# GpSimd's elementwise work in the Strassen projections of a hybrid streaming encoder goes to VectorE

## The chip, the cores and the metric

The kernel runs on one core of one Trainium2 chip. A core has five engines with a queue of instructions each, taken in order: TensorE (PE in the profile) multiplies matrices into PSUM, VectorE (DVE), ScalarE (ACT) and GpSimd (POOL) work on elements, and SyncE (SP) issues all DMAs of this kernel. The metric is the device time of one execution in microseconds (us).

## The reference, cut to what matters

Two layers over 1088 tokens (1024 of a prompt, 64 of a sample) with 1024 features in float32. The attentions and the pooling branch are not touched by the change and are left out here.

```python
def layer(x, ple, ...):
    h = rmsnorm(x, norm_in)
    hq, hkv, g_a, u_b, g_b, qkv_c, g_c, g_mix = split_cols(h @ w_in)     # input projection
    o_a, o_b, o_c = three token mixers (latent attention, pooling, chunk attention), each times silu(gate)
    gates = sigmoid(g_mix)
    m = gates[:, :D] * (o_a @ w_o_mla) + gates[:, D:2*D] * (o_b @ w_o_pool) + gates[:, 2*D:] * (o_c @ w_o_ca)
    x = x + m @ w_out                                                    # output projection
    x = x + sigmoid(rmsnorm(x, ple_norm) @ w_ple_gate) * (ple @ w_ple_proj)   # gate projection
    return x
```

## The kernel before, in words

**Tiling.** Features lie on partitions, tokens along the free dimension. Tokens are cut into two halves of H = 544, and a matmul has C = 272 columns. A float32 operand is split into a high part (float32r, a cast on ScalarE, line 108) and a low part (the operand less its high part, `lo`, lines 115 to 121), and each product is three matmuls: high by high, high by low, low by high. So every operand costs a cast on ScalarE and a subtraction on VectorE or GpSimd.

**Products.** `gemm` runs a projection as a sequence of pairs of output tiles. A pair is one level of Strassen-Winograd: seven products in the order of `PROD`, each 24 matmuls in the profile's records, of sums of weights (S1 to S4, made on VectorE in `prep_w`, line 342) with operands B11, B21, B22, T1 to T4. Weights are prepared two products ahead: sum, high part, low part (`wop`). `WLO` names the three weights of a pair (A12, S1, A22) whose low parts GpSimd makes. The running sums U2 and U3 are added on VectorE out of PSUM (line 385); U2<-P1 is the first of them in a pair, two products in, and serves below as the mark of a pair. The pairs of a layer: 22 of the input projection, then, behind the attention, 4 of the output projection and 4 of the gate projection, then the next layer's input projection. Counted through the program they are pairs 0 to 21, 22 to 25, 26 to 29, 30 to 51, 52 to 55 and 56 to 59.

**Boundaries.** The seven operands of a projection are made of four quarters of the eight tiles of x (`operand`, for each of four kb slices: scale by the gains, sum, high and low part). `OPS` gives the engine of each low part: B22 and T2 on GpSimd, B21 and T1 on both in turn where several slices come at once, the others on VectorE. `norm_boundary` (the start, the gate projections, layer 1's input projection) also runs 1/rms: squares on ScalarE, their sum in `acc` on VectorE (line 427), a matmul, a short chain, a transpose (rT), and a DMA through memory that spreads the result over all rows (`rbc`). The results of a norm boundary's products are multiplied by rbc when they leave PSUM. In the merge (`merge`), 16 blocks of the latent attention's projection are multiplied by their gate on VectorE (line 1464), added to the other two branches on GpSimd (line 1465), and turned into the operands of the output projection slice by slice, without gains.

**Order.** The program is recorded by a framework that sets the order of the instructions in each engine's queue by priorities and its own estimates; an engine does not pass over a waiting instruction. Tiles have few buffers: three PSUM buffers for products, four sums U, eighteen halves of x, three weights' operands.

**What the change touches.** `operand` (low parts, scales of line 286), `prep_w` (low parts of weights, line 353), `out` of the output projection (line 677: x + U), `out` of the gate projection (line 710: times rbc; line 714: x plus the gated addend) and `merge` (line 1465).

Of the kernel before, what the change touches and what calls it, by code (L numbers as in the profile page):

```python
# [19 lines left out]
L = 2  # L20
T = 1088            # tokens: prompt 0..1023, sample 1024..1087
H = T // 2          # token half
C = H // 2          # columns of one matmul
KT = 1600           # key tokens: prompt 1024 | cached 512 | sample 64
EPS = 1e-6
NEG = -1e30
SCALE = float(np.float32(96.0) ** np.float32(-0.5))   # of the latent attention

# z tiles (128 features each) of the input projection
# [3 lines left out]
# order of the pairs: those that are normalized lie apart  # L33
W_ORDER = (0, 4, 1, 5, 2, 6, 3, 7, 8, 9) + tuple(range(10, 22))
# gain columns
G_IN, G_PLE, G_Q, G_KV, G_KR, G_QH, G_KN, G_CQ, G_CK, G_PS, NG = 0, 8, 16, 18, 19, 20, 21, 22, 23, 24, 26
# columns that average squares
# [3 lines left out]
SECOND = 10                          # pair from which only merge gates are left  # L41
# tiles of the attention: tag, words, buffers; those that the first head waits for are apart
# [5 lines left out]
# PSUM banks of the parts of a layer  # L48
BANKS = {"gemm": (("pg", 3), ("pn", 2)), "keys": (("pg", 2), ("pn", 2), ("po", 2)),
         "attn": (("pg", 3), ("pn", 2), ("po", 1), ("pv", 2))}  # L50
LATE = 100               # how far work that fills gaps stands back
NEAR, BESIDE = 8, 14    # units before the last one at which later work is put in
PVE = ("v",)
FIRST = (2, 2, 1)         # steps of the work beside the attention that go before it
OV = 0
QC, QM = (8, 0, 1, 2, 3, 4, 5, 6, 7), (2, 3, 6, 7, 8, 0, 1, 4, 5)    # chunks of queries in order
L1, L2 = 1, 5
HEADS = tuple(("c", h) for h in range(4)) + tuple(("m", h) for h in range(8))
NRAW, NX, NZT = 3, 18, 5    # buffers: raw weights, halves of x, z tiles
# the products of an output pair: weights, operand  # L60
PROD = (("A11", "B11"), ("S2", "T2"), ("A12", "B21"), ("S3", "T3"), ("S1", "T1"), ("A22", "T4"), ("S4", "B22"))
WLO = ("A12", "S1", "A22")                         # weights whose low parts GpSimd makes
# operands in the order of their making, with the engines of their low parts
OPS = tuple(zip(("B11", "B22", "T2", "B21", "T3", "T1", "T4"), ("v", "g", "g", "vg", "v", "vg", "v")))


class Pair:
    """Two M tiles of a product: where its weights lie, where its blocks go."""

    def __init__(self, src, out, begin=None, mid=None):  # L70
        self.src, self.out, self.begin, self.mid = src, out, begin, mid


class K:
# [4 lines left out]
    # ---------------------------------------------------------------- tools  # L79
# [43 lines left out]
    def split(self, src, hi, lo, eh="a", el="v", sc=None):  # L123
        """high and low parts of src, or of src * sc"""
        self.hi(hi, src, eh, sc)
        self.lo(lo, src, hi, el, sc)
# [10 lines left out]
    # ---------------------------------------------------------------- set-up  # L137
    def setup(self, es):
# [47 lines left out]
        self.kc_d = f("kc", [2, 2, 128, KT], F32R)       # tile, hi/lo  # L186
# [4 lines left out]
    def banks(self, kind):  # L191
        """pools of PSUM banks, anew for each part of a layer"""
        if self.pes:
            self.pes.close()
        self.pes = es = ExitStack()
        for n, b in BANKS[kind]:
            setattr(self, n, es.enter_context(self.tc.tile_pool(name=n, bufs=b, space=PSUM)))
# [5 lines left out]
    # ---------------------------------------------------------------- 1/rms  # L203
    def rstd(self, sqs, col, ng, dst, w=T):
        """dst[:] <- -2/sqrt(mean square + eps) of each token, on all rows of its group; a generator."""
# [31 lines left out]
    # ---------------------------------------------------------------- operands of a Strassen-Winograd product  # L237
    def bop_tiles(self, es, side):
        """a pool for each, so that the first ones free their place before the last ones are done"""
# [5 lines left out]
    def operand(self, n, f, kbs, el, g=None):  # L245
        """operand n of the kb slices: f[kb] = (b11, b12, b21, b22), overwritten on the way; g: columns of gains"""
        nc = self.nc
        stt = nc.vector.scalar_tensor_tensor
        if n == "B11":
            self.scaled = set()  # L250
        for i, kb in enumerate(kbs):
            b11, b12, b21, b22 = f[kb]
            src = {"B11": b11, "T1": b12, "T2": b22, "B21": b21, "B22": b22, "T3": b11, "T4": b21}[n]
            e = el[i % len(el)]
# [4 lines left out]
            if n == "T2":  # L259
                if g and ("B22", kb) not in self.scaled:  # L260
# [5 lines left out]
            elif n == "T4":  # L266
                if g and ("B21", kb) not in self.scaled:
# [3 lines left out]
            if sc is not None and e == "g":  # L271
                self.scale(src, sc)
                self.scaled.add((n, kb))
                sc = None
            h, lo = (t[:, kb] for t in self.bop[n])
            self.split(src, h, lo, "a", e, sc)
            if n == "B11":
                if sc is not None:
                    self.scale(b11, g1)
                if g:  # L280
                    stt(b12, b12, g1, b11, op0=ALU.mult, op1=ALU.subtract)
# [3 lines left out]
    def scale(self, x, g):  # L285
        self.nc.gpsimd.tensor_scalar(x, x, g, 1.0, op0=ALU.mult, op1=ALU.mult)

    def operands(self, f, kbs, g=None):
        for n, el in OPS:
            self.operand(n, f, kbs, el, g)  # L290
# [5 lines left out]
    # ---------------------------------------------------------------- Strassen-Winograd over a sequence of pairs  # L296
# [3 lines left out]
    def weight_pool(self, es, side):  # L300
        """raw weights and operands of them; before the pools of the part that it is for"""
# [8 lines left out]
    def gemm_begin(self, pairs, early=()):  # L310
        """loads and first operands of the weights; early: places of sums of them"""
# [144 lines left out]
    def start(self):  # L456
        """layer 0: x from the input"""
        x = {}
# [1184 lines left out]
```

## Time and profile before

| | |
|---|---|
| median of 3 runs | 2405.88 us (2403.3 to 2421.93) |
| profiled execution, first to last instruction (span) | 2395.0 us |
| median less this span | 10.9 us |
| PE busy | 2216.3 us (93%) |
| DVE busy | 1838.6 us (77%) |
| POOL busy | 1363.5 us (57%) |
| ACT busy | 1199.8 us (50%) |

The profile records one execution. Busy shares are means over stages with different limits; the sections of the program that the change touches are read by windows of the trace further down.

### The profile page before, as it was taken

To read this page: it belongs to the slowest core of one execution; us is meant where nothing else is said; L and a number is where in the kernel's file an instruction comes from. 1 tells how busy PE (TensorE), PEld (TensorE's weight loads), DVE (VectorE), ACT (ScalarE), POOL (GpSimd) and SP (SyncE) were. 2 spreads that over 40 slices of the span, in tenths; PEclk is the share of its full clock that TensorE was granted. 3 is DMA by queue.
4 is the path that set the end of the run, shared out by engine and by line. 5 is a ranking of instruction groups with operands and counts; after the bars stand their busy time and mean duration, and the time that the engine had idled before them with its cause. 6 is when DMAs were issued, how large, how long until landed. Compare 5 with 4: busy or idle time off the path is not lost.

```text
span 2395.0 us, 44977 instructions
## 1 busy us (share of the span) xinstructions
PE 2216.3 (93%) x16134; PEld 2097.7 (88%) x16134; DVE 1838.6 (77%) x3382; ACT 1199.8 (50%) x2533; POOL 1363.5 (57%) x1326
## 2 busy tenths in 40 slices
PE   4999999999999999897869999999999999998978
PEld 3999999999778999797859999999987789997978
DVE  8666787675677888889996667877756778888897
ACT  5334355454666665344443343654546766743442
POOL 6544545667455545657775354447564555455677
PEclk8999999999899999998969999999989999999989
DMA  3433446355966664434515344554478656655253
GB/s 112 173 117 125 161 151 195 118 163 176 252 186 176 189 184 152 169 131 136 193 59 182 113 143 163 163 155 148 137 201 244 183 171 181 178 178 174 91 164 120
DMA packets 234610, 383.59 MB, mean 160 GB/s; under 512 B 30020, under 2 KB 130708, under 8 KB 234388
## 3 DMA queue, kind: packets, MB, share of 16 engines
q1 hardware_dynamic: 234388, 380.72, 51.0%
q8 instruction: 129, 2.11, 0.4%
q14 instruction: 93, 0.76, 0.1%
HBM read 245.94 MB, written 134.70 MB: 159 GB/s over the span
## 4 chain that ended last, share of the span: by engine, by line
PE 61%; DVE 17%; DMA 7%; issue 7%; POOL 5%; ACT 3%; SPq 1%; POOLq 0%; DVEq 0%; ACTq 0%
PE g L377 35%; PE S L1065 4%; PE pv L884 4%; PE pT L850 4%; PE S L994 3%; DVE S L342 2%; DVE wop L119 2%; PE mps L130 1%; DVE acc L427 1%; PE mps L132 1%; PE mps L131 1%; PE vps L1034 1%; DMA of<-mbo 1%; PE turn L1110 1%; DMA of<-p 1%
## 5 line engine op out<-in xcount | busy, mean ns | idle before, releaser
L644 POOL TENSOR_TENSOR z<-z,rbc 128x544 f32<-128x544 f32 x134 | 207.3, 1551 | 178.4 <-DVE z L643 168.3
L119 POOL TENSOR_TENSOR wop<-wraw,wop 128x512 fp32r<-128x512 f32 (+1 forms) x152 | 208.9, 1375 | 141.1 <-ACT wop L108 138.8
L824 POOL TENSOR_SCALAR P<-P,st 128x640 f32<-128x640 f32 (+8 forms) x216 | 155.2, 722 | 218.6 <-DVE st L823 135.0
L108 ACT CAST wop<-wraw 128x512 fp32r<-128x512 f32 (+1 forms) x230 | 138.7, 604 | 218.2 <-PE g L377 159.9
L108 ACT CAST wop<-S 128x512 fp32r<-128x512 f32 x234 | 144.7, 619 | 164.1 <-PE g L377 156.7
L119 DVE TENSOR_TENSOR wop<-S,wop 128x512 fp32r<-128x512 f32 x176 | 170.0, 966 | 72.0 <-ACT wop L108 70.7
L377 PE MATMUL g<-T1h,wop 128*128 128x272 f32 x960 | 183.6, 304 | 21.3 <-DVE U L385 19.0
L377 PE MATMUL g<-B11h,wop 128*128 128x272 f32 x960 | 176.1, 295 | 18.0 <-ACT B11h L110 11.7
L119 DVE TENSOR_TENSOR PT<-pT,PT 128x512 fp32r<-128x512 f32 (+4 forms) x360 | 167.9, 473 | 30.0 <-ACT PT L108 27.6
L377 PE MATMUL g<-B21h,wop 128*128 128x272 f32 x960 | 181.3, 299 | 9.4 <-ACT P L389 5.3
L377 PE MATMUL g<-T3h,wop 128*128 128x272 f32 x960 | 180.3, 297 | 7.4 <-ACT T3h L108 4.9
L377 PE MATMUL g<-T2h,wop 128*128 128x272 f32 x960 | 178.6, 296 | 8.9 <-ACT T2h L108 6.6
L108 ACT CAST PT<-pT 128x512 fp32r<-128x512 f32 (+4 forms) x360 | 147.7, 419 | 67.2 <-PE pT L850 61.3
L377 PE MATMUL g<-B22h,wop 128*128 128x272 f32 x960 | 172.8, 290 | 7.5 <-DVE U L385 4.7
L377 PE MATMUL g<-T4h,wop 128*128 128x272 f32 x960 | 172.6, 291 | 2.1 <-DVE ev L704 2.1
L884 PE MATMUL pv<-PT,V 128*128 128x256 f32 x928 | 167.3, 301 | 6.0 <-DVE PT L119 5.4
L130 PE MATMUL mps<-oh,wop 128*128 128x272 f32 x512 | 157.1, 308 | 16.2 <-DVE g L1464 9.2
L377 PEld LDWEIGHTS g<-T1h,wop 128*128 128x128 f32 x960 | 150.3, 202 | 24.5 <-issue 14.3
L850 PE MATMUL pT<-ident,P 128*128 128x128 f32 x936 | 160.0, 279 | 3.1 <-DVE PT L119 2.7
L1065 PE MATMUL S<-K,Q 96*128 96x384 f32 (+5 forms) x672 | 158.6, 353 | 3.4 <-ACT P L816 3.3
L377 PEld LDWEIGHTS g<-B11h,wop 128*128 128x128 f32 x960 | 143.6, 194 | 19.4 <-ACT B11h L110 12.0
L377 PEld LDWEIGHTS g<-B21h,wop 128*128 128x128 f32 x960 | 146.7, 196 | 13.3 <-ACT P L389 7.9
(274 smaller groups left out, 6957.0 us busy)
## 6 DMA issues: line engine op xcount, KB each, us to landing
wraw<-win SPq DMA_DIRECT2D x88, 512.0 KB
z<-z SPq DMA_DIRECT2D x96, 272.0 KB
g<-z SPq DMA_DIRECT2D x64, 272.0 KB
z<-z SPq DMA_DIRECT2D x24, 544.0 KB
Q<-q SPq DMA_DIRECT2D x32, 408.0 KB
K<-k SPq DMA_DIRECT2D x32, 400.0 KB
k<-hl SPq DMA_DIRECT2D x48, 256.0 KB
q<-hl SPq DMA_DIRECT2D x64, 192.0 KB
```

Source lines behind the costliest of these rows:

```text
L108: nc.scalar.copy(out, src)
L119: e.tensor_sub(out, src, hi)
L130: mm(ps, lhsT=wh, rhs=xh, start=first, stop=False)
L131: mm(ps, lhsT=wh, rhs=xl, start=False, stop=False)
L342: op(tmp[nm], x, y)
L377: nc.tensor.matmul(ps[:, c, :C], lhsT=hl[:, w, kb, :], rhs=b[:, kb, c * C:(c + 1) * C], start=k == 0 and not more, stop=k == 11, skip_grou ...
L644: nc.gpsimd.tensor_mul(o, o, self.half(self.r, ti))
L824: nc.gpsimd.tensor_scalar(u.p[:, :n], u.p[:, :n], st[:, 4:5], 1.0, op0=ALU.mult, op1=ALU.mult)
L850: nc.tensor.transpose(ps[:, j], p[:, c0:c0 + 128], self.ident)
L884: nc.tensor.matmul(ps[:, :w], lhsT=v(b), rhs=grp[b // 4][:, b % 4, j, :w], start=i + j == 0, stop=i == len(bl) - 1 and j == 1)
L994: nc.tensor.matmul(ps[:, :w], lhsT=q[:, q0:q0 + 128], rhs=k[:q.shape[0], k0 + c * w:k0 + c * w + w], start=q is q1, stop=q is q2)
L1065: nc.tensor.matmul(ps[:, :ww], lhsT=q[0:96, q0:q0 + 128], rhs=k[0:96, k0 + c * w:k0 + c * w + ww], start=i == 0, stop=i == 2 and not diag)
```

## The change

Five kinds of GpSimd instructions go to VectorE: the low parts of the operands at all boundaries, the low parts of the weights A12, S1 and A22 in the output and gate projections and in the first two pairs of each input projection (`calm` is true from the third pair on, where they stay), x + U in the output projection, the two elementwise operations of the gate projection, and the addition in the merge. The scales by gains, which were separate GpSimd instructions, are taken into the instruction that makes the low part or the sum, but for that of B11, which ScalarE does.

```diff
-WLO = ("A12", "S1", "A22")                         # weights whose low parts GpSimd makes
-# operands in the order of their making, with the engines of their low parts
-OPS = tuple(zip(("B11", "B22", "T2", "B21", "T3", "T1", "T4"), ("v", "g", "g", "vg", "v", "vg", "v")))
+WLO = ("A12", "S1", "A22")
+
+OPS = ("B11", "B22", "T2", "B21", "T3", "T1", "T4")
...
-                if g and ("B22", kb) not in self.scaled:
+                if g:
                     stt(b22, b22, g2, b12, op0=ALU.mult, op1=ALU.subtract)
...
-                if g and ("B21", kb) not in self.scaled:
+                if g:
                     stt(b21, b21, m2, b22, op0=ALU.mult, op1=ALU.add)
...
-            if sc is not None and e == "g":
-                self.scale(src, sc)
-                self.scaled.add((n, kb))
-                sc = None
             h, lo = (t[:, kb] for t in self.bop[n])
-            self.split(src, h, lo, "a", e, sc)
+            self.split(src, h, lo, "a", "v", sc)
             if n == "B11":
-                if sc is not None:
-                    self.scale(b11, g1)
                 if g:
+                    nc.scalar.activation(b11, b11, AF.Copy, scale=g1)
                     stt(b12, b12, g1, b11, op0=ALU.mult, op1=ALU.subtract)
...
-        self.split(src, hl[:, 0], hl[:, 1], "a", "g" if n in WLO else "v")
+        self.split(src, hl[:, 0], hl[:, 1], "a", "g" if n in WLO and pairs[p].calm else "v")
...
             if sb is not None:
-                nc.gpsimd.tensor_add(o, o, sb)
+                nc.vector.tensor_add(o, o, sb)
...
-                nc.gpsimd.tensor_mul(t, t, self.half(self.r, ti))
+                nc.vector.tensor_mul(t, t, self.half(self.r, ti))
...
-            nc.gpsimd.tensor_add(o, o, g)
+            nc.vector.tensor_add(o, o, g)
...
-                nc.gpsimd.tensor_add(self.half(mb, ti), self.half(mb, ti), self.half(g, ti))
+                nc.vector.tensor_add(self.half(mb, ti), self.half(mb, ti), self.half(g, ti))
```

The queues change as follows: VectorE has 238 instructions more, GpSimd 278 fewer, ScalarE 16 more; TensorE's count is the same. In the rows below, names are tiles of the program with their buffer numbers, and the line numbers of the changed kernel differ (385 is 374, 1464 is 1453, 1465 is 1454, 678 is 667, 677 is 666, 709 is 698, 710 is 699, 713 is 702).

VectorE at the head of layer 0's merge, before (g0 is a gate, mps the projection in PSUM, mb the sum of the other branches):

```order
L1464 TENSOR_TENSOR g0_11903<-g0_11903,mps_11909 128x544
L1464 TENSOR_TENSOR g0_11903<-g0_11903,mps_11936 128x544
L119 TENSOR_TENSOR wop_12050<-wraw_12048,wop_12050 128x512
L1464 TENSOR_TENSOR g0_11907<-g0_11907,mps_11972 128x544
L119 TENSOR_TENSOR B11l_11867<-mb_11901,B11h_11866 128x544
L283 TENSOR_TENSOR mb_11901<-mb_11901 128x544
```

The same place now:

```order
L1453 TENSOR_TENSOR g0_11897<-g0_11897,mps_11903 128x544
L1453 TENSOR_TENSOR g0_11897<-g0_11897,mps_11930 128x544
L1454 TENSOR_TENSOR mb_11895<-mb_11895,g0_11897 128x544
L119 TENSOR_TENSOR wop_12044<-wraw_12042,wop_12044 128x512
L1454 TENSOR_TENSOR mb_11895<-mb_11895,g0_11897 128x544
L1453 TENSOR_TENSOR g0_11901<-g0_11901,mps_11966 128x544
L119 TENSOR_TENSOR B11l_11861<-mb_11895,B11h_11860 128x544
L275 TENSOR_TENSOR mb_11895<-mb_11895 128x544
```

The additions to mb stand in VectorE's queue between the gates now. From the first of these rows to the next projection's first U2<-P1 there were 67 instructions on VectorE, and there are 93.

VectorE at the end of the boundary from the output to the gate projection, and the first products behind it, before (rt is the copy of the transposed 1/rms ahead of its DMA, ev the gate's block, x the addend and the stream):

```order
L226 COPY rt_13563<-rT_13561 9x128
L119 TENSOR_TENSOR T4l_11892<-x_12986,T4h_11891 128x544
L342 TENSOR_TENSOR S2_13846<-S1_13844,wraw_13663 128x512
L385 TENSOR_TENSOR U3_13725<-U2_13656,g_13700 128x544
L119 TENSOR_TENSOR wop_13766<-S4_13764,wop_13766 128x512
L119 TENSOR_TENSOR wop_13806<-wraw_13663,wop_13806 128x512
L385 TENSOR_TENSOR U2_13656<-U2_13656,g_13730 128x544
L709 TENSOR_TENSOR ev_13756<-U3_13725,g_13730 128x544
L342 TENSOR_TENSOR S3_13924<-wraw_13663 128x512
L709 TENSOR_TENSOR ev_13796<-U3_13725,g_13771 128x544
L119 TENSOR_TENSOR wop_13848<-S2_13846,wop_13848 128x512
L713 TENSOR_TENSOR x_13569<-x_13569,ev_13689 128x544
```

The same place now:

```order
L226 COPY rt_13551<-rT_13549 9x128
L374 TENSOR_TENSOR U3_13713<-U2_13644,g_13688 128x544
L119 TENSOR_TENSOR wop_13794<-wraw_13651,wop_13794 128x512
L331 TENSOR_TENSOR S3_13912<-wraw_13651 128x512
L374 TENSOR_TENSOR U2_13644<-U2_13644,g_13718 128x544
L698 TENSOR_TENSOR ev_13744<-U3_13713,g_13718 128x544
L698 TENSOR_TENSOR ev_13784<-U3_13713,g_13759 128x544
L119 TENSOR_TENSOR wop_13836<-S2_13834,wop_13836 128x512
L699 TENSOR_TENSOR ev_13677<-ev_13677,rbc_87 128x544
L699 TENSOR_TENSOR ev_13744<-ev_13744,rbc_87 128x544
L699 TENSOR_TENSOR ev_13784<-ev_13784,rbc_87 128x544
L702 TENSOR_TENSOR x_13557<-x_13557,ev_13677 128x544
```

The three products with rbc, which stood in GpSimd's queue, stand in VectorE's eight instructions behind the copy that starts rbc's DMA.

## Rows read from the trace of the kernel before

**Rows 1.** The page: the span, and busy time of each engine (share, instructions).

```profile
span 2395.0 us, 44977 instructions
PE 2216.3 (93%) x16134; PEld 2097.7 (88%) x16134; DVE 1838.6 (77%) x3382; ACT 1199.8 (50%) x2533; POOL 1363.5 (57%) x1326
```

**Rows 2.** Windows: start:end, length, busy us and instructions of each engine, clock, DMA.

```profile
core 0: us, PE busy (x) PEld busy (x) DVE busy (x) ACT busy (x) POOL busy (x), PEclk, DMA share, GB/s
9.80:63.40 53.60, 29.75 (x109) 24.54 (x110) 50.07 (x55) 29.53 (x50) 43.12 (x24) 0.80 0.22 83
63.40:97.80 34.40, 34.40 (x267) 34.37 (x267) 21.96 (x28) 12.94 (x20) 21.92 (x15) 0.96 0.60 211
937.20:1005.30 68.10, 56.46 (x412) 53.61 (x410) 66.04 (x68) 24.52 (x41) 44.96 (x27) 0.97 0.44 149
1038.70:1059.70 21.00, 21.00 (x170) 21.00 (x169) 15.91 (x20) 7.50 (x12) 10.76 (x8) 1.00 0.29 104
1044.80:1067.90 23.10, 23.10 (x187) 23.10 (x186) 19.27 (x24) 11.16 (x18) 14.01 (x11) 1.00 0.27 95
1067.90:1116.60 48.70, 36.28 (x218) 34.09 (x218) 48.50 (x51) 23.26 (x40) 39.61 (x22) 0.79 0.36 116
1116.60:1192.10 75.50, 66.82 (x507) 64.98 (x504) 70.09 (x70) 31.64 (x52) 53.96 (x35) 0.98 0.56 186
1192.10:1252.70 60.60, 37.64 (x186) 34.21 (x186) 60.57 (x58) 27.47 (x47) 49.55 (x30) 0.66 0.19 64
2128.50:2196.50 68.00, 56.59 (x413) 53.73 (x412) 65.96 (x68) 24.53 (x41) 45.02 (x27) 0.97 0.51 177
2236.00:2259.10 23.10, 23.10 (x185) 23.10 (x184) 19.05 (x23) 10.70 (x18) 13.70 (x11) 1.00 0.26 94
2259.10:2307.90 48.80, 36.19 (x220) 34.26 (x219) 48.80 (x50) 23.68 (x39) 39.72 (x22) 0.79 0.37 115
2307.90:2374.30 66.40, 62.51 (x493) 61.41 (x492) 55.70 (x59) 22.87 (x38) 47.39 (x31) 1.00 0.47 158
2386.10:2395.00 8.90, 0.02 (x1) 0.00 (x0) 2.59 (x3) 0.96 (x2) 5.31 (x4) 0.76 0.25 94
```

**Rows 3.** Waits of PE, 1083 to 1262 us: who for whom, total, times, longest.

```profile
PE g L377 <- DVE T3l L119: 9.8, 3, 6.4
```

**Rows 4.** Timeline, DVE near the start: start us, duration us, instruction.

```profile
33.53 0.71 DVE L427 TENSOR_TENSOR acc<-acc,sq 128x544 f32<-128x544 f32 x1
34.16 0.71 DVE L263 TENSOR_TENSOR x<-x 128x544 f32<-128x544 f32 x1
...
35.43 0.77 DVE L281 SCALAR_TENSOR_TENSOR x<-x,gh 128x544 f32<-128x544 f32 x1
36.13 0.68 DVE L119 TENSOR_TENSOR wop<-S,wop 128x512 fp32r<-128x512 f32 x1
36.73 0.71 DVE L265 TENSOR_TENSOR x<-x 128x544 f32<-128x544 f32 x1
```

**Rows 5.** Timelines of DVE, then of POOL, at the boundary to the gate projection.

```profile
1098.98 1.87 DVE L270 TENSOR_TENSOR x<-x 128x544 f32<-128x544 f32 x1
1100.77 1.85 DVE L263 TENSOR_TENSOR x<-x 128x544 f32<-128x544 f32 x1
...
1098.44 1.83 POOL L119 TENSOR_TENSOR B22l<-x,B22h 128x544 fp32r<-128x544 f32 x1
1100.23 1.81 POOL L119 TENSOR_TENSOR T2l<-x,T2h 128x544 fp32r<-128x544 f32 x1
```

**Rows 6.** Groups by line: instruction, count, busy us, mean ns, idle before it.

```profile
L385 DVE TENSOR_TENSOR U<-U,g 128x544 f32<-128x544 f32 x120 | 85.7, 715 | 49.5 <-PE g L377 49.0
L342 DVE TENSOR_TENSOR S<-wraw 128x512 f32<-128x512 f32 x118 | 112.3, 951 | 40.9 <-POOL wop L119 37.1 <-DMA wraw<-win 1.6 <-DMA wraw<-wout 0.9
L1465 POOL TENSOR_TENSOR mb<-mb,g 128x544 f32<-128x544 f32 x32 | 54.3, 1706 | 44.6 <-DVE g L1464 44.6
L710 POOL TENSOR_TENSOR ev<-ev,rbc 128x544 f32<-128x544 f32 x26 | 43.2, 1671 | 33.3 <-DVE ev L709 17.7 <-DMA rbc<-rd 15.5
```

**Rows 7.** Timelines of DVE, then of POOL: the copy that starts rbc's DMA, its first use.

```profile
1119.23 0.27 DVE L226 COPY rt<-rT 9x128 f32<-9x128 f32 x1
...
1126.54 4.00 POOL L710 TENSOR_TENSOR ev<-ev,rbc 128x544 f32<-128x544 f32 x3 [7.79 <-DMA rbc<-rd]
```

More of the change, by code (lines that the diff above doesn't have):

```diff
@@ L62, with __init__ @@
 WLO = ("A12", "S1", "A22")
-OPS = tuple(zip(("B11", "B22", "T2", "B21", "T3", "T1", "T4"), ("v", "g", "g", "vg", "v", "vg", "v")))
+OPS = ("B11", "B22", "T2", "B21", "T3", "T1", "T4")
 class Pair:
-    def __init__(self, src, out, begin=None, mid=None):
-        self.src, self.out, self.begin, self.mid = src, out, begin, mid
+    def __init__(self, src, out, begin=None, mid=None, calm=False):
+        self.src, self.out, self.begin, self.mid, self.calm = src, out, begin, mid, calm
 class K:
@@ L243, in bop_tiles, with operand @@
             self.bop[n] = tuple(p.tile([128, 4, H], F32R, name=f"{n}{s}") for s in "hl")
-    def operand(self, n, f, kbs, el, g=None):
+    def operand(self, n, f, kbs, g=None):
         nc = self.nc
         stt = nc.vector.scalar_tensor_tensor
-        if n == "B11":
-            self.scaled = set()
-        for i, kb in enumerate(kbs):
+        for kb in kbs:
             b11, b12, b21, b22 = f[kb]
             src = {"B11": b11, "T1": b12, "T2": b22, "B21": b21, "B22": b22, "T3": b11, "T4": b21}[n]
-            e = el[i % len(el)]
             g1 = g2 = m2 = sc = None
@@ L283, in operand @@
                     nc.vector.tensor_sub(b12, b12, b11)
-    def scale(self, x, g):
-        self.nc.gpsimd.tensor_scalar(x, x, g, 1.0, op0=ALU.mult, op1=ALU.mult)
     def operands(self, f, kbs, g=None):
-        for n, el in OPS:
-            self.operand(n, f, kbs, el, g)
+        for n in OPS:
+            self.operand(n, f, kbs, g)
     @staticmethod
@@ L448, in norm_boundary @@
         g = (self.gh[l], gcol), (self.gh[l], gcol + 4), (self.gm[l], gcol + 4)
-        for n, el in OPS:
-            self.operand(n, f, range(4), el, g)
+        for n in OPS:
+            self.operand(n, f, range(4), g)
             if n in ("B11", "T2"):
@@ L658, in pair @@
             return Pair(lambda kh: d["win"][l, p, kh], lambda *a: out(2 * p, *a), {0: start, SECOND: second}.get(i),
-                        lambda j: self.fill(2 if i < SECOND else 1))
+                        lambda j: self.fill(2 if i < SECOND else 1), i > 1)
         return [pair(i, p) for i, p in enumerate(W_ORDER)], lambda: S["es"].close()
```

## The prediction

> **What bounds the kernel now.** The page comes first: TensorE is busy 93% of the span, VectorE 77%, GpSimd 57% [rows 1]. By these shares a move from GpSimd to VectorE looks like a move from the freer engine to the fuller one, so the share has to be read where the change is made. The second view is the table of windows [rows 2]. Its row from 1038.7 shows one pair of the output projection in its steady state: 21.00 us, TensorE busy in all of it at full clock, VectorE in 15.91. There VectorE has room, and what is moved costs nothing. The other rows are the boundaries. In the start (9.8 to 63.4) TensorE is busy 29.75 of 53.60 us and VectorE 50.07; in the merge VectorE is busy 66.04 of 68.10; in the boundary to the gate projection 48.50 of 48.70; in that to layer 1's input projection 60.57 of 60.60, with TensorE at 37.64 and a granted clock of 0.66. So VectorE sets the pace at every boundary, and the waits say it too: between 1083 and 1262 the largest group is TensorE waiting for VectorE's T3l, 9.8 us [rows 3].
>
> The third view is the timeline, and it decides the case. With GpSimd idle, VectorE's instructions on two SBUF operands follow each other after 0.63 us (128x544), 0.70 (with a scalar) and 0.60 (128x512) [rows 4]. At the boundary the same instructions last 1.85 and 1.87 us, and the starts of VectorE's and GpSimd's alternate every 1.8 us: each waits for the other [rows 5]. An instruction with an operand in PSUM is not drawn out: U has a mean of 715 ns over 120, while S, from SBUF alone, has 951 over 118 [rows 6]. So VectorE's busy time at the boundaries is in good part waiting for GpSimd, and an instruction moved over takes about 0.63 us of VectorE's time and gives back up to 1.2 us (1.87 less 0.63) to whatever ran beside it.
>
> **The change part by part.** GpSimd loses 278 instructions: 60 low parts of weights (30 a layer), 64 low parts of operands (12 at each of four norm boundaries, 8 in each merge), 40 scales, 32 additions of the merge, 24 of x + U, 26 products with rbc, 32 additions of the gated addend. ScalarE gains 16 scales; it is busy 23 to 32 us in windows of 49 to 76 [rows 2], so these are hidden, and were it full they would cost 16 by some 0.6 us. The other 24 scales go into instructions that VectorE runs anyway. VectorE gains the remaining 238. SyncE's DMAs are the same ones, and only those at the boundaries stand in another order.
>
> I make the sum stage by stage: the instructions on VectorE in the order of the changed program, at the undisturbed distances [rows 4] (0.635, 0.70 and 0.60 us, the short ones of the chain 0.15), plus an allowance for waits, against the window before [rows 2]. Where TensorE needs longer, its 21.0 us a pair stand instead.
>
> Start: 52 instructions on VectorE, from the first B11l to the last T3l, become 64 (33 by 0.635, 24 by 0.70, 7 by 0.60: 42.0 us). I add the 3.5 us that VectorE idled before (53.60 less 50.07): 45.5, a gain of 8.1. The next window is TensorE's: 267 matmuls at 21.00/170 each are 33.0 of 34.4, so at most 1.4, and I take 1.0.
>
> Merge: 67 instructions become 93 (76 by 0.635, 17 by 0.60: 58.5). With the 2.1 us of idle time of before 60.6 against 68.1 and 68.0: 7.5 and 7.4.
>
> Output projection into the gate's boundary (1044.8 to 1116.6, 71.8 us in two windows, 71.9 in layer 1): TensorE's pair of 21.0, then VectorE's 49 instructions between the last pair's mark and the gate's first become 73 (34 by 0.635, 20 by 0.70, 16 by 0.60, 3 short: 45.7). With 1.5 for waits, 68.2: 3.6 and 3.7.
>
> Gate projection of layer 0 (1116.6 to 1192.1, 75.5 us): 69 instructions become 87 (53.9 us), less than TensorE's three pairs of 63.0. Here the change adds a wait on VectorE: rbc arrives 7.3 us after the copy that starts its DMA (1126.54 less 1119.23 [rows 7]). GpSimd waited for it before, with 7.79 us idle; now VectorE does, eight instructions behind the copy. Those eight hold T1's and A22's blocks, so VectorE comes there some 6 us after the copy and stands about 1 us. Behind the wait are the block of the last product, the gated addends and the next pair's A12; TensorE needs that one only two products later (6 us), so the wait stays off its path. With 2.5 us for this and the sigmoids, 65.5: a gain of 10.0.
>
> Boundary to layer 1's input projection (1192.1 to 1252.7, 60.6 us): 57 instructions become 90 (49 by 0.635, 23 by 0.70, 15 by 0.60, 3 short: 56.7); with 2.0 for waits 58.7: 1.9. Little is won here: GpSimd's share was large, and all of it now stands in one queue.
>
> Gate projection of layer 1 (66.4 us): 58 become 84 (51.9), TensorE 63.0, with 1.5 for waits 64.5: 1.9. The tail behind the last product is 8.90 us, of which GpSimd's four instructions take 5.31; two of them on the path go from some 1.4 to 0.7: 1.5.
>
> The sum is 8.1 + 1.0 + 14.9 + 7.3 + 10.0 + 1.9 + 1.9 + 1.5 = 46.6 us. 2395.0 - 46.6 = 2348.4 us of span, and with the 10.9 us that lie between the span and the median of the runs, **2359 us**.
>
> Bounds. The trace of before shows no stage in which VectorE runs this fast against ScalarE's casts for long. With no wait at all the terms are 11.6, 1.4, 9.6 + 9.5, 5.1 + 5.2, 12.5, 3.9, 3.4 and 2.0, 64 us: 2342. With waits of a tenth of VectorE's time the start gains 3.9 (42.0 becomes 46.2, plus 3.5), the merges 1.6 and 1.5 (66.5), the two output boundaries 0.5 each (71.3), the gate projections, at 23 us a pair, 6.5 and -2.6, the boundary to layer 1 -1.8, the tail 1: 11 us, 2395. I take little waiting, because the stretch from 33.5 to 36.7 us [rows 4] ran back to back amid the same casts; 657 instructions in these stages make each 1% of waiting worth some 5 us (64 less 11, by 10).
>
> **Rivals.** *Waits between ScalarE and VectorE.* T2, T3 and T4 of a slice are a chain: sum on VectorE, cast on ScalarE, low part on VectorE. At a third of the old durations the cast may no longer be done in time, and VectorE stands. That is the case of a tenth: 2395 us, within 1% of now. Against it stands that the order puts other slices' instructions between.
>
> *VectorE is full, and what is added is added.* In this case the long durations are VectorE's own, and the moved instructions come on top of its busy time [rows 2]: 12 in the start (+4.5 us beyond the window), 26 in each merge (66 + 16.5 is 82.5, +14.4 twice), 24 before each gate projection (48.5 + 15.4 is 63.9, +15.2 twice), 18 in layer 0's gate projection (+6.0), 33 in the boundary to layer 1 (60.6 + 21.2, +21.2), 26 in layer 1's gate projection (55.7 + 16.5 is 72.2, +5.8): 97 us, 2503. The point that decides is the mean distance of VectorE's instructions in these stages: 490 us of windows over 657 instructions is 0.745 us; below it the change gains, above it loses. For it speaks only the busy share; against it the pairs 0.71 and 1.87 us for the same instruction [rows 4, 5], and U, which runs beside GpSimd undrawn [rows 6]. The Trainium skill, in Perfetto Trace Analysis, Optimizing Scalar/DVE Operations, says that a saturated VectorE may be worth relieving through ScalarE or even GpSimd, which speaks against this change; by that alone the time would be this rival's. It adds that the two share an SBUF read port, so that moving work between them may not help; the 1.87 us in this trace bear that second part out.
>
> *Nothing moves.* TensorE hides all of it: 2406. Against it, TensorE idles in every boundary window.
>
> **How the numbers follow.** The forecast has 0.79, the waits 0.15, the full VectorE 0.04, no change 0.02. The range goes from the sum without waits, 2341, to 2389, about an eleventh of VectorE's time spent waiting, and leaves out 2 in 10 at most. A measurement of this kernel tells about 1% (24 us) from no change. Faster by more than that, below 2382, holds most of the forecast and a little of the waiting: 0.82; within it 0.14; slower 0.04.
>
> **What would show it.** In the changed profile VectorE's x, mb, S and low parts at the boundaries should take 0.68 to 0.78 us, GpSimd should be idle there, the last T3l of the start should end by 56 us, a merge should take 60 to 61 us from its first gate to U2<-P1, and layer 0's gate projection about 65 us. The sum is wrong if VectorE shows idle time before low parts (waiting for ScalarE's casts) or before the products with rbc beyond some 2 us a boundary, or if a steady pair of the gate projection takes over 22 us.

## The result, and the profile after

The changed kernel takes 2344.05 us (median of 4 runs, 2342.63 to 2348.71) against 2405.86 of the kernel before beside it (2403.3 to 2421.93): a ratio of 0.9742, 95% interval 0.9714 to 0.977. The forecast was 2359, from 2341 to 2389; the direction held and the gain, 61.8 us, came out larger than the 46.6 forecast. The profiled execution went from 2395.0 to 2341.1 us. The page of the changed kernel, which answers to [rows 1]:

```profile
span 2341.1 us, 44783 instructions
PE 2207.0 (94%) x16134; PEld 2091.4 (89%) x16134; DVE 1801.4 (77%) x3620; ACT 1216.7 (52%) x2549; POOL 908.9 (39%) x1048
```

VectorE has 238 instructions more and is busy for 37 us less. The windows of the changed kernel that answer to [rows 2] (columns as there): the start up to the last T3l, the merge, the output projection's third pair, the boundary from there to the gate projection, the gate projection, the boundary to layer 1, then layer 1's merge and gate projection.

```profile
9.50:52.10 42.60, 26.26 (x106) 22.36 (x107) 42.10 (x65) 31.48 (x52) 0.00 (x0) 0.83 0.30 111
937.20:996.40 59.20, 55.38 (x412) 54.41 (x412) 58.55 (x94) 23.72 (x40) 0.00 (x0) 0.94 0.50 173
1033.40:1054.30 20.90, 20.90 (x170) 20.90 (x169) 18.80 (x29) 10.95 (x18) 0.00 (x0) 1.00 0.32 105
1054.30:1099.60 45.30, 36.99 (x256) 35.04 (x255) 45.30 (x73) 27.88 (x45) 0.00 (x0) 0.92 0.43 136
1099.60:1156.40 56.80, 56.80 (x442) 56.44 (x441) 54.14 (x89) 27.54 (x45) 0.00 (x0) 0.98 0.64 208
1156.40:1212.80 56.40, 40.91 (x231) 37.59 (x230) 56.40 (x92) 34.10 (x55) 0.00 (x0) 0.75 0.30 98
2097.40:2157.70 60.30, 54.95 (x407) 53.74 (x407) 58.82 (x93) 23.50 (x39) 0.00 (x0) 0.94 0.57 196
2261.50:2319.00 57.50, 57.15 (x442) 56.83 (x441) 52.81 (x86) 21.82 (x35) 0.00 (x0) 0.97 0.55 178
```

GpSimd has nothing to do in any of them. VectorE is still what is full at the boundaries, but it gets through 65 to 94 instructions in less time than through 51 to 70 before. VectorE's timeline at the boundary to the gate projection (answers to [rows 5]) shows why:

```profile
1078.80 1.48 DVE L258 SCALAR_TENSOR_TENSOR x<-x,gh 128x544 f32<-128x544 f32 x2
1080.19 0.68 DVE L119 TENSOR_TENSOR wop<-S,wop 128x512 fp32r<-128x512 f32 x1
1080.80 0.72 DVE L262 TENSOR_TENSOR x<-x 128x544 f32<-128x544 f32 x1
1081.43 0.78 DVE L265 SCALAR_TENSOR_TENSOR x<-x,gm 128x544 f32<-128x544 f32 x1
1082.13 0.72 DVE L119 TENSOR_TENSOR T2l<-x,T2h 128x544 fp32r<-128x544 f32 x1
```

The instructions that took 1.85 and 1.87 us there follow each other every 0.6 to 0.7 us. Counted through the traces by shape of output, 296 of VectorE's 1456 instructions on 128x544 or 128x512 lasted over 1 us before, and 95 of 1694 do now.

### The profile page after: what moved, and what is told of

It is laid out like the page before. It is cut to its first block, busy times and chain, and to the rows that moved or that the text cites. A ratio compares the mean times of both kernels' runs of the same rounds, so it can differ in the third digit from the quotient of the medians.

```text
span 2341.1 us, 44783 instructions
## 1 busy us (share of the span) xinstructions
PE 2207.0 (94%) x16134; PEld 2091.4 (89%) x16134; DVE 1801.4 (77%) x3620; ACT 1216.7 (52%) x2549; POOL 908.9 (39%) x1048
## 4 chain that ended last, share of the span: by engine, by line
PE 63%; DVE 16%; DMA 8%; issue 5%; ACT 3%; POOL 3%; SPq 1%; POOLq 0%; DVEq 0%; ACTq 0%
PE g L366 38%; PE pv L873 4%; PE pT L839 4%; PE S L1054 3%; PE S L983 3%; DVE wop L119 1%; DMA g<-z 1%; PE mps L130 1%; PE vps L1023 1%; PE mps L132 1%; DVE S L331 1%; PE mps L131 1%; DMA of<-mbo 1%; PE turn L1099 1%; DMA r<-rd 1%
## 5 line engine op out<-in xcount | busy, mean ns | idle before, releaser
L119 POOL TENSOR_TENSOR wop<-wraw,wop 128x512 fp32r<-128x512 f32 (+1 forms) x112 | 148.5, 1327 | 120.5 <-ACT wop L108 119.2
L366 PE MATMUL g<-B11h,wop 128*128 128x272 f32 x960 | 175.3, 293 | 18.0 <-ACT B11h L110 13.3
L366 PEld LDWEIGHTS g<-B11h,wop 128*128 128x128 f32 x960 | 142.4, 191 | 19.9 <-ACT B11h L110 14.1
L366 PEld LDWEIGHTS g<-T3h,wop 128*128 128x128 f32 x960 | 145.9, 194 | 14.1 <-ACT T3h L108 13.5
```

The source lines that it names most:

```text
L119: e.tensor_sub(out, src, hi)
L366: nc.tensor.matmul(ps[:, c, :C], lhsT=hl[:, w, kb, :], rhs=b[:, kb, c * C:(c + 1) * C], start=k == 0 and not more, stop=k == 11, skip_grou ...
```

## The experiments

Two theories. **Exclusion:** a VectorE instruction with both operands in SBUF and a GpSimd instruction that reads SBUF can't run at once; what is moved gives back more than it costs. **Length alone:** each engine's time is its own, and the gain came from shorter instructions and fewer waits between engines.

**GpSimd's load without its work.** The changed kernel, with 96 subtractions on GpSimd that nobody waits for:

```diff
             self.split(src, h, lo, "a", "v", sc)
+            if n in ("B22", "T2", "B21", "T1"):
+                nc.gpsimd.tensor_sub(self.scr, h.bitcast(F32), lo.bitcast(F32))
```

> The changed kernel with 96 GpSimd subtractions added that nobody waits for: one behind each low part of B22, T2, B21 and T1 (16 at each of the six boundaries), reading the high and the low part from SBUF and writing a scratch tile. VectorE's queue is that of the changed kernel. Theory (VectorE and GpSimd exclude each other when both work on SBUF): VectorE's instructions beside them go from 0.71 to 1.2 to 1.9 us, each subtraction costs VectorE 0.7 to 1.2 us, and the time is 2344 + 60 to 110 us = 2404 to 2454. Rival (the gain came from shorter work and fewer waits between engines, and GpSimd does not disturb VectorE): 0.71 us as now, 2344 within 10.

Measured: 2399.55 us, ratio to the kernel before 0.998 (0.9957 to 1.0003). That is just under the 2404 to 2454 expected; the whole gain is gone, though all of the work stands where the change put it. Timelines of this kernel at the gate's boundary, VectorE's, then GpSimd's:

```profile
1098.72 1.89 DVE L419 TENSOR_TENSOR acc<-acc,sq 128x544 f32<-128x544 f32 x1
...
1106.46 0.71 DVE L263 TENSOR_TENSOR x<-x 128x544 f32<-128x544 f32 x1
1107.09 1.87 DVE L266 SCALAR_TENSOR_TENSOR x<-x,gm 128x544 f32<-128x544 f32 x1
1108.88 0.77 DVE L276 SCALAR_TENSOR_TENSOR x<-x,gh 128x544 f32<-128x544 f32 x1
```

```profile
1098.24 1.79 POOL L272 TENSOR_TENSOR scr<-B22h,B22l 128x544 f32<-128x544 f32 x1 [1.42 <-DVE B22l L121]
1106.05 2.33 POOL L272 TENSOR_TENSOR scr<-T2h,T2l 128x544 f32<-128x544 f32 x1 [6.01 <-DVE T2l L119]
```

The subtraction of 1106.05 stands while VectorE runs the instruction of 1106.46 at 0.71; the next one takes 1.87. So one GpSimd instruction can draw out one VectorE instruction by about 1.1 us (1.87 against 0.77 for this kind). Not each of them does: 175 instructions last over 1 us in this kernel, 80 more than in the changed one, for 96 subtractions, and VectorE's busy time grows by 80.0 us, from the 1801.4 above, or 0.83 us a subtraction. (The 110 us in an expectation below are 96 by 1.15, not a measurement.) The page of this kernel:

```profile
PE 2222.3 (93%) x16134; PEld 2102.6 (88%) x16134; DVE 1881.4 (79%) x3620; ACT 1215.0 (51%) x2549; POOL 1117.8 (47%) x1144
```

**Busy, but not reading.** The same places, each subtraction replaced by a read of one column and two memsets:

```diff
+                nc.gpsimd.tensor_scalar(self.scr[:, :1], lo[:, :1].bitcast(F32), 1.0, 1.0, op0=ALU.mult, op1=ALU.mult)
+                nc.gpsimd.memset(self.scr, 0.0)
+                nc.gpsimd.memset(self.scr, 0.0)
```

> As the run with 96 subtractions, but each is replaced by a read of one column of the low part and two memsets of the same 128x544 scratch tile, so GpSimd is busy for about as long and at the same places, but reads next to nothing. Theory that reads from SBUF are what collides: VectorE stays at 0.71 us and the time within 10 us of 2344. Theory that any access of GpSimd to SBUF holds VectorE up: VectorE at 1.2 us and more, 2404 to 2454 as with the subtractions.

Measured: 2350.26 us (2344.03 to 2364.08), ratio 0.9769 (0.9713 to 0.9825). VectorE's timeline with GpSimd's memsets beside it:

```profile
1081.52 0.72 DVE L672 TENSOR_TENSOR x<-x,g 128x544 f32<-128x544 f32 x1
1082.15 0.79 DVE L121 SCALAR_TENSOR_TENSOR B21l<-x,gh,B21h 128x544 fp32r<-128x544 f32 x1
```

```profile
1081.72 0.55 POOL L273 MEMSET scr<- 128x544 f32 x1
1082.33 0.55 POOL L274 MEMSET scr<- 128x544 f32 x1
1082.96 2.65 POOL L272 TENSOR_SCALAR scr<-B22l 128x1 f32<-128x1 f32 x1
```

VectorE stays at 0.72 and 0.79 beside memsets; the read of a single column lasts 2.65 us. GpSimd is busy for 1141.2 us in this kernel, more than with the subtractions (1117.8), at the same places and behind the same low parts. So it is GpSimd's reading, not its being busy or its place in the order, that draws VectorE out. The Trainium skill, SBUF — State Buffer, Who interferes with whom, says the same: a VectorE instruction with two inputs in SBUF contends with a GpSimd instruction that reads SBUF, not with one that only writes it. Both runs agree, and so does U with its one operand in PSUM, 715 ns before [rows 6] and 713 now.

**One part undone at a time**, from the changed kernel: the operands' low parts and scales as before; the low parts of weights; the elementwise work of the output and gate projections; the addition in the merge.

```diff
-OPS = ("B11", "B22", "T2", "B21", "T3", "T1", "T4")
+OPS = tuple(zip(("B11", "B22", "T2", "B21", "T3", "T1", "T4"), ("v", "g", "g", "vg", "v", "vg", "v")))
...
-        self.split(src, hl[:, 0], hl[:, 1], "a", "g" if n in WLO and pairs[p].calm else "v")
+        self.split(src, hl[:, 0], hl[:, 1], "a", "g" if n in WLO else "v")
...
-                nc.vector.tensor_add(o, o, sb)
+                nc.gpsimd.tensor_add(o, o, sb)
...
-                nc.vector.tensor_add(self.half(mb, ti), self.half(mb, ti), self.half(g, ti))
+                nc.gpsimd.tensor_add(self.half(mb, ti), self.half(mb, ti), self.half(g, ti))
```

> The changed kernel with the operands of the boundaries as before: 64 low parts and 40 scales back on GpSimd, 64 instructions fewer on VectorE. Theory (exclusion): each GpSimd instruction draws one VectorE instruction out by 1.15 us (1.86 less 0.71, as the 96 subtractions did), and each low part gives VectorE back 0.635 us: 64 by 0.5 and 40 by 1.15 are 79 us of VectorE's time; of the subtractions' 110 us the span kept 51, so by the same share 36 us: 2344 + 25 to 45 = 2369 to 2389. Rival (no disturbance, VectorE's length alone counts): 64 by 0.635 us less on VectorE, 41 us, and the time falls below 2344.

> The changed kernel with the 60 low parts of weights back on GpSimd in the output and gate projections and the first two pairs of the input projections. Theory (exclusion): 60 by 0.5 us, 31 us of VectorE's time, more than half of it under TensorE's steady pairs: 5 to 15 us slower than the changed kernel, 2349 to 2359. Rival (VectorE's length alone): 2335 to 2344.

> The changed kernel with x + U of the output projection and the two elementwise operations of the gate projection back on GpSimd (82 instructions). Theory (exclusion): 82 by 0.5 us, 42 us of VectorE's time, of which the boundaries to the gate projection and to layer 1's input projection keep about 40%: 10 to 22 us slower, 2354 to 2366. Rival (VectorE's length alone): 2330 to 2344.

> The changed kernel with the 32 additions of the merges back on GpSimd. Theory (exclusion): 32 by 0.5 us is 16 us of VectorE's time, in merges that VectorE sets: 5 to 12 us slower, 2349 to 2356, both merges 3 to 6 us longer than 59.2 and 60.3. Rival (VectorE's length alone): VectorE gets 16 by 0.635 us shorter in each merge, 2330 to 2344.

Measured: 2375.05 us (ratio 0.9848, 0.9828 to 0.9867) with the operands undone, 2348.93 (0.9732, 0.971 to 0.9755) with the weights, 2359.63 (0.9781, 0.9761 to 0.9801) with the elementwise work, 2359.99 (0.9786, 0.976 to 0.9812) with the merge's addition. Three became slower and none became faster beyond the noise, so length alone falls.

The medians alone overstate these prices, because the kernel before took 2411.58 us beside these runs and 2405.86 beside the changed kernel. By the ratios the operands cost 25.5 us, the elementwise work 9.4, the merge's addition 10.6, and the weights nothing (-2.4, where 5 to 15 were expected); by the medians it is 31.0, 15.6, 15.9 and 4.9. The intervals leave each price by ratio open by some 8 or 9 us either way. The merge's time of 2359.99 missed the 2349 to 2356 expected, its price by ratio did not.

Where each stretch stands against the changed kernel, in us of the profiled executions (two numbers: layers 0 and 1). "Start to third pair" runs from the span's start to the third pair's mark, "merges" from the first gate to the next mark, "into gate's boundary" from the third output pair's mark to the gate projection's first, "gate projections" from their first mark to their fourth, and "boundary to layer 1" from there to layer 1's first mark:

| | start to third pair | merges | into gate's boundary | gate projections | boundary to layer 1 |
|---|---|---|---|---|---|
| changed kernel | 95.7 | 59.2, 60.3 | 66.3, 66.5 | 56.7, 57.5 | 56.4 |
| 96 subtractions | +12.5 | +5.4, +4.3 | +9.4, +8.9 | +3.5, +1.6 | +10.6 |
| memsets | +1.2 | +1.3, -1.3 | +0.2, -0.2 | +0.2, -0.4 | 0.0 |
| operands undone | +8.4 | +2.4, +0.8 | +6.0, +5.9 | +0.7, -2.6 | +8.6 |
| weights undone | -0.7 | +1.6, +0.3 | +1.4, +1.2 | +5.1, +1.9 | -2.5 |
| elementwise undone | +2.1 | -0.2, +0.1 | +1.5, +1.4 | +14.1, +5.4 | -3.6 |
| merge undone | +1.2 | +5.7, +4.6 | +0.2, -0.2 | -0.2, 0.0 | +0.6 |

Each part is worth its gain in its own stretch: the operands at every norm boundary, the elementwise work in the gate projections. The weights are not told from nothing. The merge's addition is worth 10.3 us in the merges themselves, which agrees with the 10.6 by ratio.

**More of the same.** The exclusion is still at work beside the gates of the input projection: the seventh pair, here from its first matmul to the next pair's, took 28.6 us, and one product of VectorE in it 3.00. First the low parts of weights of pairs 5 to 9 went to VectorE, then the gates' products with rbc there too, then the low parts of weights of all other pairs besides.

```diff
-                        lambda j: self.fill(2 if i < SECOND else 1), i > 1)
+                        lambda j: self.fill(2 if i < SECOND else 1), i > 1 and not 5 <= i <= 9)
...
-                nc.gpsimd.tensor_mul(o, o, self.half(self.r, ti))
+                (nc.vector if Z_GA <= m < Z_MIX else nc.gpsimd).tensor_mul(o, o, self.half(self.r, ti))
```

> The changed kernel with the low parts of A12, S1 and A22 on VectorE in the pairs 5 to 9 of each input projection too (the ones with gates z times sigmoid; 30 instructions). In the trace of the changed kernel the 7th and 9th pair of a layer take 28.6 and 26.9 us (28.4 and 27.3 in layer 1) where TensorE needs some 21, with VectorE's products at 1.6 us beside GpSimd. Theory (the same exclusion is still at work there): 5 to 15 us faster than the changed kernel, 2329 to 2339. Rival (VectorE, busy 22.8 to 24.3 us in such a pair, is full, and what is added is added): 2 us more in each of these four pairs, 2344 to 2355.

> As the run before it, and the products of the gates with rbc in the same pairs go to VectorE as well (24 to 30 more). Theory (exclusion): no GpSimd instruction but the low parts of keys is left beside VectorE there; 10 to 25 us faster than the changed kernel, 2319 to 2334. Rival (VectorE full): 26 VectorE instructions a pair become 33, 4 us more in each of the four pairs, 2350 to 2365.

> The changed kernel with all low parts of weights on VectorE in every pair (102 more beyond the ones in the change) and the products of the gates with rbc in pairs 5 to 9 too. Against the kernel that has this in pairs 5 to 9 alone (2329.6): theory (exclusion; the other pairs are TensorE's, busy in all of 21 to 26 us): no difference, 2324 to 2334. Rival (VectorE becomes full in the pairs beside keys and queries, where it is busy 15 to 22 us in 23 to 26): 1 us more in twenty-four pairs, 2345 to 2360.

Measured: 2335.36 us (0.9692, 0.9656 to 0.9728), 2329.56 (0.9668, 0.9629 to 0.9707) and 2330.14 (0.9683, 0.9646 to 0.9719). The seventh pair in the changed kernel, and in the second of the three (columns as in [rows 2]), with VectorE's product in each:

```profile
185.50:214.10 28.60, 24.48 (x171) 23.91 (x170) 22.81 (x23) 9.14 (x14) 19.32 (x10) 0.88 0.57 193
```

```profile
198.60 3.00 DVE L642 TENSOR_TENSOR z<-z,sg 128x544 f32<-128x544 f32 x1
```

```profile
186.10:209.30 23.20, 21.51 (x170) 21.13 (x169) 20.96 (x26) 7.70 (x13) 7.58 (x4) 1.00 0.63 216
```

```profile
189.44 0.71 DVE L642 TENSOR_TENSOR z<-z,sg 128x544 f32<-128x544 f32 x1
```

VectorE runs three instructions more and is busy 1.9 us less; the pair is 5.4 us shorter. All three came as the exclusion forecast. The third step adds nothing that can be measured: the other pairs are TensorE's. The second and third are the fastest kernels of this case, below both that were given.

**The clock at the head of the attention.** Here no instruction was moved, and yet the profile of the changed kernel is longer there. TensorE's windows from the last input pair's mark to the merge's first gate, before:

```profile
575.10:937.20 362.10, 347.14 (x2392) 304.54 (x2391) 268.87 (x820) 233.40 (x659) 185.14 (x264) 0.97 0.69 194
1762.10:2128.40 366.30, 349.43 (x2390) 305.82 (x2389) 270.70 (x821) 233.38 (x659) 184.82 (x264) 0.96 0.68 192
```

and in the changed kernel:

```profile
568.00:937.20 369.20, 350.09 (x2389) 305.98 (x2389) 270.56 (x820) 234.06 (x659) 185.50 (x264) 0.96 0.68 190
1724.90:2097.40 372.50, 355.24 (x2394) 309.84 (x2392) 270.54 (x820) 234.03 (x660) 185.30 (x264) 0.95 0.68 189
```

Same work, 7.1 and 6.2 us longer. The granted clock falls to 0.5, that is 1.2 GHz, some 19 us behind the mark, where TensorE stands waiting for operands of the addend's products (in the changed kernel 3.15 us, for ScalarE's cast of oh, at 589.7). The low clock adds up to 20.5 and 27.3 us in the two stretches before, 30.7 and 37.5 now, and 54.6 in the longest of the first ten profiles (377.4 us). To see whether the clock is the cause, products there were computed more than once:

```diff
-                for k in range(2):
+                n = 5 if (m, ti, c) == (0, 0, 1) else 2 if (m, ti) > (0, 0) and m < 3 else 1
+                for k in (0, 1) * n:
```

> The changed kernel with the first products of the addend's projection (pps) beside the head of each attention computed more than once into the same place: the second one five times, the next ten twice, 14 groups of six matmuls more per layer, some 10 us of TensorE at full clock. In ten profiles so far the granted clock falls to 0.5 some 19 us behind the mark of a layer's last input pair, for 10 to 41 us, and the stretch from that mark to the merge's first gate lasts 362 us (20.5 us at the low clock in it) to 377 us (54.6). Theory (the low clock lengthens the head of the attention, and it falls because TensorE stands there): under 10 us at the low clock in the head, both stretches at 358 to 364 us, the time 2328 to 2340. Rival (the head waits for loads and for the chain through ScalarE and VectorE, the low clock is only a sign of it): the clock stays up, the stretches stay at 367 to 375 us, 2344 to 2350.

> Pairs 5 to 9 with nothing but keys' low parts on GpSimd, together with the repeated products at the head of the attention. If both theories hold, their gains add: 2329.6 less 4 to 16 us, 2314 to 2326. If the low clock is only a sign: 2329 to 2335.

> The kernel with all low parts of weights and the gates' products with rbc on VectorE (2330.1), and of the addend's products only the seven groups that fall into the head of the attention repeated (the second five times, the third to seventh twice: 9 groups more a layer). The run that repeated eleven groups kept the clock up in the head and came 3 to 7 us earlier to the 41st score matmul, but then repeated four groups in a stretch where TensorE is busy, stood for 2.9 us there with the clock down again, and lost the gain and more. Theory (the low clock does lengthen the head, and repeating where TensorE stands costs nothing): the two stretches from the last input pair's mark to the merge at 358 to 364 us, the time 2314 to 2325. Rival (what is won in the head is lost behind it, whatever is repeated): stretches as without, 365 to 375 us, 2328 to 2336.

Measured: 2353.22 us, 2338.78 with the second version above, and 2331.99 for the shorter set of repeats on the third (2330.14 without). The first kernel's windows of the attention:

```profile
568.00:942.10 374.10, 355.13 (x2473) 315.59 (x2472) 271.06 (x820) 233.60 (x659) 183.86 (x264) 0.98 0.67 188
1732.30:2110.50 378.20, 360.16 (x2479) 318.92 (x2477) 271.96 (x821) 234.18 (x660) 183.68 (x264) 0.96 0.67 187
```

The clock did stay up in the head (3.4 us low there, not 20.5): filling the time in which TensorE stood was enough, so one half of the theory is borne out, that it falls because TensorE stands. The 31st score matmul (an expectation miscounts it as the 41st) came 43.9 us after the mark, not 50.8, and 44.5, not 47.9. But TensorE is busy 95% of this stretch, and 84 more matmuls, 10.4 us at 21.0/170 each, are not free: by the 41st score matmul the lead is 0.8 us in layer 0 and a lag of 4.0 in layer 1, and the stretches came out 4.9 and 5.7 us longer, though the clock was low for some 14 and 10 us less. None of the three gains came. The first two kernels missed both of their expected ranges, with medians 9.2 us above those without repeats; the intervals of the ratios overlap, so of the times only "no gain" is shown. The third fell into its rival's range, with stretches of 369.6 and 365.0 us beside 365.0 and 367.1.

The traces say more when taken together. In the 22 such stretches of the eleven profiles without repeats, the length follows the time at the low clock: 356.4 us, and 0.38 us more for each us at 0.5 (a straight line fitted here; correlation 0.95, no stretch more than 2.2 us off it). The six stretches with repeats lie above that line, by 7.6 to 13.4 us for 84 more matmuls (10.4 us) and by 4.7 and 6.7 us for 54 (6.7 us). So the repeated products are paid for about in full. A correlation does not say which of the two causes the other; the earlier 31st score matmul speaks for the clock. What makes the low clock of the head last 20 us in one execution and 41 in another stays open.

## Why the prediction was right, and where it was off

**Mechanism.** Right: the runs with added subtractions and with memsets show it, and the marks came as named (VectorE's instructions at 0.68 to 0.78 us, GpSimd idle, the last T3l at 52.1 us, the merges at 59.2 and 60.3), all but the gate projection's 65 us. Full VectorE, 2503 us, and no change fell at once. One reading was off: of the stretch in [rows 4], GpSimd is idle only up to 35.02 us. From there it has an instruction under way, while VectorE's behind it still take 0.68 to 0.77:

```profile
35.02 5.43 POOL L286 TENSOR_SCALAR x<-x,gh 128x544 f32<-128x544 f32 x1 [3.90 <-ACT sq L426]
```

The price of 0.63 us holds all the same; the changed kernel has it at the boundaries, where GpSimd is idle throughout.

**Stage by stage**, gains in us of the profiled executions:

| stretch | forecast | measured |
|---|---|---|
| start to last T3l; from there to the third pair | 8.1; 1.0 | 10.9; -3.0 |
| merges | 7.5 + 7.4 | 8.9 + 7.7 |
| first two output pairs | 0 | 2.6 + 2.7 |
| into the gate's boundary | 3.6 + 3.7 | 5.4 + 5.3 |
| gate projection, layers 0 and 1 | 10.0 + 1.9 | 18.8 + 9.1 |
| boundary to layer 1 | 1.9 | 4.3 |
| last pair; tail | 0; 1.5 | -3.0; 1.1 |
| everything else | 0 | -16.9 |
| sum | 46.6 | 53.9 |

**Waits.** The allowance was too large: VectorE is busy 42.10 of 42.60 us in the start and all of the boundary to layer 1. The start, the merge of layer 0, the boundaries into the gate and that to layer 1 lie within 0.7 us of the sum without waits (gains of 11.6, 9.6, 5.1, 5.2 and 3.9). Layer 1's merge is 1.8 short of its 9.5. The rival of waits between ScalarE and VectorE did not come.

**The gate projections are the step that failed**, 27.9 us measured for 11.9. The forecast set TensorE's three pairs, 63.0 us, as a floor between the first and the fourth mark. The mark is VectorE's instruction, and at the first one VectorE is behind: part of the three pairs' products is already done. Between the marks lie 442 matmuls now (507 before), not 510; at 21.0/170 us each that is 54.6 us, and VectorE's own sum, forecast as 53.9, is 54.14. Both lie 2 to 3 us below the 56.8 measured (the clock stood at 0.5 up to 1102.4 us, and VectorE idled 2.7). The floor was counted in pairs where it should have been counted in matmuls. The last pair's loss of 3.0 us is the other side of this: the window behind the last mark holds 115 matmuls now and 88 before, 3.3 us of TensorE. The 5.3 us of the first two output pairs, put at nothing, are not explained here.

**The wait for rbc** on VectorE came as forecast, a bit longer, 2.29 us where some 1 was named; TensorE shows no gap from it (busy 56.80 of 56.80 us). VectorE's timeline of the changed kernel:

```profile
1100.88 0.27 DVE L226 COPY rt<-rT 9x128 f32<-9x128 f32 x1
...
1108.24 2.00 DVE L699 TENSOR_TENSOR ev<-ev,rbc 128x544 f32<-128x544 f32 x3 [2.29 <-DMA rbc<-rd]
```

**The 10.9 us "around the span" were misread.** Every run gives its time beside its span, and they lie 1.7 to 2.4 us apart (2342.89 and 2341.1 for the changed kernel). The profiled execution of before was simply short: 2395.0 us, where 13 other executions have spans from 2396.8 to 2420.6. Its attention in layer 0, 362.1 us, is shorter than in any of thirteen other profiles.

So not all of the 16.9 us that the profiles lose in "everything else" is the change's. The profile of before lies about 9 us below its median execution, that of the changed kernel about 1: some 8 us belong to which execution was profiled. That is also what the fitted line gives for the two attentions, 20.5 us more at the low clock by 0.38, of the 13.3 that they lose. Another 3.6 us are lost in the input pairs, where GpSimd still works; the rest is open, for there is only one profile of the kernel before.

In sum: 24.2 us too little in the stretches that change, 16.9 too much in those that don't, 9.1 too much around them: 2359 - 24.2 + 16.9 - 9.1 is 2342.6, beside 2342.89 for the profiled execution. The number is in part luck. The changed stretches gained 70.8 us, more than the 64 of the sum without waits that was to be the bound, and the total came into the range only because the other stretches lost a part of it again (16.9 between the profiles, some 9 by the medians).

## What to carry to other kernels

Before reading VectorE's busy share as work, compare one instruction's duration beside an idle and a busy GpSimd: here 0.71 and 1.87 us, and an instruction moved to a "full" VectorE cost 0.63 us and gave back up to about 1.1 (0.83 in the mean, by the 96 subtractions). Where a floor is set by an engine, count its instructions between the very marks that are compared. And one profiled execution can lie 9 us from the median; compare unchanged stretches first.

## What was not expected of the hardware

In [rows 5] the two engines take turns. They do not always: with VectorE's queue full and few instructions on GpSimd, GpSimd waits. In the kernel with the subtractions the one below lasts 5.52 us, and VectorE runs six instructions at 0.68 to 0.72 us beside it before one takes 1.89:

```profile
1111.07 5.52 POOL L272 TENSOR_TENSOR scr<-T2h,T2l 128x544 f32<-128x544 f32 x1 [2.69 <-DVE T2l L119]
```

```profile
1114.65 0.71 DVE L119 TENSOR_TENSOR T3l<-x,T3h 128x544 fp32r<-128x544 f32 x1
1115.29 1.89 DVE L259 SCALAR_TENSOR_TENSOR x<-x,gh 128x544 f32<-128x544 f32 x1
```

The subtractions behind T2 took 3.2 us in the mean and the one-column reads behind B22 2.9 us, while memsets took 0.55. What decides between turns and waiting is not shown. These groups (columns as in [rows 6]), subtractions, then reads and memsets:

```profile
L272 POOL TENSOR_TENSOR scr<-T2h,T2l 128x544 f32<-128x544 f32 x24 | 76.2, 3176 | 89.2 <-DVE T2l L119 76.2 <-DVE chain L221 12.5
```

```profile
L272 POOL TENSOR_SCALAR scr<-B22l 128x1 f32<-128x1 f32 x24 | 68.6, 2856 | 269.2 <-DVE B22l L121 228.8 <-DVE B22l L119 39.4
L273 POOL MEMSET scr<- 128x544 f32 x96 | 53.1, 553 | 5.5
```
